# A two-layer hybrid decoder step on one core: the second part of the tokens as one 512-column product, gate_a through Silu

## The chip, the core and the metric

The kernel runs on one core of a Trainium2 chip. The core has five engines with an instruction queue each, and each queue runs strictly in its order: PE (TensorE, the matrix products; PEld is its loading of weights), DVE (VectorE), ACT (ScalarE), POOL (GpSimd) and SP (here the queue that issues most transfers). Matrix products land in PSUM; DVE and ACT read them from there. The metric is the device time of one launch in microseconds (us), smaller is better; times of single instructions are also given in nanoseconds (ns).

## The reference

One inference step of two layers over 512 prompt tokens and 8 sample tokens, all in float32, with 1024 channels. Per layer:

```python
h = rms_norm(x, norm_g)
z = h @ w_in                       # 50 blocks of 128 columns: glu 16, k, v, q 8, gate_b 8, mg_b 8, mg_a 8 (and gate_a 8)
u = glu[..., :1024] * sigmoid(glu[..., 1024:])
c = conv(concat([conv_buf, u]), conv_w) + conv_b           # 31 taps, each channel by itself
c = silu(layer_norm(c, ln_g, ln_b)) * silu(gate_a)
y_a = c @ w_conv_out
o, new_k, new_v = attend(rope(q), rope(k), v, sinks)       # window of 128, 16 heads, 2 kv heads
y_b = (o * silu(gate_b)) @ w_attn_out
y = sigmoid(mg_a) * y_a + sigmoid(mg_b) * y_b
x = x + y @ w_out
```

After the two layers comes a last rms_norm. The last 30 conv inputs and the last 128 keys and values go out too.

## The kernel before

Channels lie on the partitions and the 520 tokens along the free axis, so that an activation is 8 tiles of 128 x 520. Weights come in blocks of 1024 x 128. One such block with its product over all tokens is a `Unit`; there are 82 in a layer, 164 in all: 16 GLU, K, V, 8 Q, 8 gate_b (GB), 16 merge gates (MB, MA), 8 gate_a (GA), 8 YB, 8 YA, 8 OUT.

To hold float32 accuracy with products of the reduced type `fp32r`, weights and activations are split into a high and a low part (`whi` and `wlo`; a pair of tiles for each activation), and three products are summed: high x high, low weight x high, high weight x low activation. `Unit.__init__` loads the weights over SP (`raw`), ACT casts them to `whi` (line 109) and DVE subtracts to get `wlo` (line 110). `raw` has two buffers, `whi` and `wlo` three each. The tokens are done in two halves of 260; each half of a unit is 8 blocks of input channels times 3 products of 260 columns, 48 in a unit, all on line 124, into one PSUM bank per half. `mm` pairs of banks exist twice, so the results of a unit have to be read before the next unit but one begins. A single ACT copy or DVE operation over 520 columns does that, according to the unit's kind.

The attention of a layer goes in 32 steps (`scores`, `transposes`, `values`), with half a unit of MB or MA between two steps. The depthwise convolution is 240 DVE operations per layer (line 563, 30 taps for each of 8 tiles) with a low priority, put in wherever DVE has room. Its end is followed by a layer norm: a sum over channels, which is a matrix product with `ones` (line 160, reading `ssum`), the subtraction of the mean (577), squares, a second sum, then the scale (581), Silu (602) and the product with gate_a (604). The result is needed by the YA units.

The order on each engine is written by a list scheduler when the program is built. It works with its own estimates of time and the priorities; on the chip each queue is then fixed, and an instruction whose input is late holds up everything behind it in its queue.

Of the kernel before, what the change touches and what calls it, by code (L numbers as in the profile page):

```python
# [19 lines left out]
HALF = TOK // 2  # L20
# [23 lines left out]
def hybrid_step(ctx, tc, x_in, w_in, par, const, rope, conv_st, kc_in, vc_in,  # L44
# [6 lines left out]
    gp = ctx.enter_context(tc.tile_pool(name="gp", bufs=42))  # L51
# [16 lines left out]
    def g(dt=F32):  # L68
        return gp.tile([128, TOK], dt, tag="g", name=name("g"))

    def og(dt=F32):
        return gp.tile([128, TOK], dt, tag="o", bufs=16, name=name("o"))

    def two(t):
        return t.rearrange("p (a b) -> p a b", a=2)
# [18 lines left out]
    def split(src, n=TOK, new=g):  # L94
        hi, lo = new(F32R), new(F32R)
        A.copy(hi[:, :n], src)
        mark[0] = V.tensor_tensor(lo[:, :n], src, hi[:, :n].bitcast(F32), op=ALU.subtract)  # L97
        return hi, lo

    class Unit:  # L100


        def __init__(self, l, idx, hs, los, spare=False):
            self.hs, self.los = hs, los
# [6 lines left out]
            if spare:  # L111
                banks = [psT.tile([128, 512], F32, tag="T", name=name("T")),
                         psV.tile([128, 512], F32, tag="V", name=name("V"))]
                self.acc = [b[:, :HALF] for b in banks]
# [12 lines left out]
        def half(self, hf):  # L127
            for k in range(KT):
                self.step(hf, k)
            return self.acc[hf]  # L130

        def both(self):
            self.half(0)
            self.half(1)
            return self.ps

    class Sum:
# [6 lines left out]
        def add(self, i, v, halves=(0, 1)):  # L144
            if i == 7 and len(halves) == 1:
                self.left[halves[0]] = two(v)[:, halves[0], :]
                return
            c = slice(halves[0] * HALF, (halves[-1] + 1) * HALF)
# [8 lines left out]
        def total(self, hf):  # L157
            ps = sbank()[:, :HALF]
            last = self.left.get(hf)
            PE.matmul(ps, ones, two(self.acc)[:, hf, :], start=True, stop=last is None)  # L160
# [7 lines left out]
    def rstd(sums, halves=(0, 1)):  # L168
        y0, v, a = tmp("y0", 1), tmp("v", 1), tmp("a", 1)
        c = slice(halves[0] * HALF, (halves[-1] + 1) * HALF)  # L170
        for hf, s in zip(halves, sums):
            h = slice(hf * HALF, (hf + 1) * HALF)
# [22 lines left out]
    def first_units(l):  # L195
        return [Unit(l, W_GLU, xh, xl), Unit(l, W_GLU + 1, xh, xl)]

    def rows(x, i):

        w = pt[:, P_G + i:P_G + i + 1]  # L200
        a, b = g(F32R), g(F32R)
        A.mul(a, x, w)  # L202
        mark[0] = V.scalar_tensor_tensor(b, x, w, a.bitcast(F32), op0=ALU.mult, op1=ALU.subtract)
        xh.append(a)
        xl.append(b)
# [5 lines left out]
    xs, xh, xl, sq = [], [], [], Sum()  # L211
    first = []
    xt = [g() for _ in range(KT)]
    for i in range(KT):
        if i < 2:
            first.append(Unit(0, W_GLU + i, xh, xl))
# [6 lines left out]
    for l in range(L):  # L223
# [6 lines left out]
        hh, hl = [], []  # L230

        def normed(lo, hi):
            for i in range(lo, hi):
# [3 lines left out]
                a, b = split(h)  # L237
                hh.append(a)
                hl.append(b)
# [3 lines left out]
        for i in range(KT):  # L243
            if i % 2 == 0:
# [3 lines left out]
            src = (xh, xl) if i < EARLY else (hh, hl)  # L248
            if i == 0:
                for k in range(KT):  # L250
                    for u in first:
                        u.step(0, k)
                        u.step(1, k)
                R = rstd(sq.totals())
                a, b = first
            else:
                a = Unit(l, W_GLU + 2 * i, *src, spare=(i == 1))
                a.half(0)
                a.half(1)
            u = up.tile([128, PAD + TOK], F32, tag="u", name=f"u{l}_{i}")  # L260
            G.memset(u[:, :PAD], 0.0)
            uu = two(u[:, PAD:])
            sg = g()
            if i < EARLY:
                for hf in range(2):
                    A.copy(two(sg)[:, hf, :], a.acc[hf])
                if i > 0:
                    b = Unit(l, W_GLU + 2 * i + 1, *src)
                    b.both()
                A.copy(uu, b.ps)  # L270
# [4 lines left out]
                V.tensor_tensor(uu, uu, two(sg), op=ALU.mult)  # L275
            else:
                A.activation(two(sg), a.ps, AF.Sigmoid)
                z1 = Unit(l, W_GLU + 2 * i + 1, *src).both()
                V.tensor_tensor(uu, z1, two(sg), op=ALU.mult)
# [23 lines left out]
        kps = Unit(l, W_K, hh, hl).both()  # L303
        kn, kcos, ksin, krot = g(), g(), g(), g()
        nc.gpsimd.dma_start(kcos, rope[2])
        nc.gpsimd.dma_start(ksin, rope[3])
        A.copy(two(kn), kps)
        V.tensor_tensor(krot, kn, kcos, op=ALU.mult)
        vps = Unit(l, W_V, hh, hl).both()
        vt = g()  # L310
        A.copy(two(vt), vps)
        nc.gpsimd.dma_start(nvp[l], vt[:, T - 128:T])
        for hf in range(2):
            c = slice(hf * HALF, (hf + 1) * HALF)
            kss = sbank()
            PE.matmul(kss[:, :HALF], swap, kn[:, c], start=True, stop=True)
            V.tensor_tensor(ksin[:, c], kss[:, :HALF], ksin[:, c], op=ALU.mult)
# [3 lines left out]
        for kv in range(2):  # L321
            a, b = g(F32R), g(F32R)
# [8 lines left out]
        for j in range(2):  # L331
            t = g()
# [9 lines left out]
        cosx, sinx = g(), g()  # L342
# [3 lines left out]
        def q_store(e, src):  # L346
            a, b = split(src[:, :T], T)
            for j, t in ((0, a), (HD, b)):
                nc.sync.dma_start(qscr[:, j + 8 * e:j + 8 * e + 8, :], t[:, :T].bitcast(F32))
            nc.gpsimd.dma_start(qsam[:, 8 * e:8 * e + 8, :], src[:, T:])  # L350

        x1p = Unit(l, W_Q, hh, hl).both()
        x1, x1c, x1s = g(), g(), g()
        A.copy(two(x1), x1p)
# [6 lines left out]
        vb = g()  # L361
# [3 lines left out]
        vrow = g()  # L365
# [4 lines left out]
        for j in range(2):  # L370
            t = g()
# [6 lines left out]
        x2p = Unit(l, W_Q + 1, hh, hl).both()  # L378
        x2, x2c, x2s = g(), g(), g()
        A.copy(two(x2), x2p)  # L380
        for e in range(2, 8):
            q = Unit(l, W_Q + e, hh, hl).both()
            qe = tmp("sq", 3)
            A.copy(two(qe), q)
# [8 lines left out]
        qn = g()  # L393
        qn3 = qn[:, :128].rearrange("p (t v n) -> p t v n", t=8, v=2)
        G.memset(qn[:, :128], 0.0)
# [7 lines left out]
        def load_q(t):  # L403
            for kv in range(2):
                q = g(F32R)
                nc.sync.dma_start(q[:, :T].bitcast(F32), qscr[2 * t + kv])
                qs[t, kv] = q

        sgb = []
        for t in range(8):  # L410
            ps = Unit(l, W_GB + t, hh, hl).both()
            s = g()
            A.activation(two(s), ps, AF.Silu)  # L413
            sgb.append(s)
# [7 lines left out]
        def sample_scores():  # L422
            ss = sbank()
            for j in range(2):
                qb = g()
                G.memset(qb[:, :512], 0.0)
                qb3 = qb[:, :512].rearrange("p (n m) -> p n m", n=4)
                for n in range(4):
                    nn = 4 * j + n
                    V.tensor_copy(qb3[:, n, nn * 16:nn * 16 + 16],  # L430
                                  qn[:, :128].rearrange("p (h n) -> p h n", n=NS)[:, :, nn])
                    PE.matmul(ss[:, :128], qb3[:, n, :], kc[j][:, n, :],  # L432
                              start=(nn == 0), stop=(nn == 7))
            ns = g()
# [356 lines left out]
```

## Time and profile before

| | |
|---|---|
| time of three runs | 1074.34 to 1075.82 us, median 1075.18 |
| the profiled execution's own time | 1074.0 us |
| its span from the first to the last instruction | 1072.2 us |
| granted TensorE clock, mean | 0.997 of full speed |
| PE busy | 1053.9 us, 98% of the span |
| DVE busy | 854.2 us, 80% |
| ACT busy | 514.0 us, 48% |

A share of busy time is an average over stages. Products are pipelined on PE: the record of one lasts longer than the distance to the next one's start, and this distance (its pitch) is what a product costs in a dense run. The same holds on a smaller scale on DVE.

### The profile page before, as it was taken

Reading aid. Unit: us, or ns where it says so; the run is one execution under the profiler, and the core shown is the slowest. Engines: PE = TensorE matmul, PEld = TensorE weight load, DVE = VectorE, ACT = ScalarE, POOL = GpSimd, SP = SyncE. Lnnn points to the kernel's source line nnn. Section 1 sums busy time; section 2 is a strip of 40 time slices with the busy share of each in tenths; the row PEclk is TensorE's granted clock in tenths of the full one; section 3 lists DMA queues with packets and bytes.
Section 4 is the critical chain, followed back from the end, with each engine's and each line's share of the span. In section 5 each row is a group of like instructions: output and inputs, shape, how many; then the busy total and the mean of one; then the engine's idle time right before and its main releaser. Section 6 shows DMA issues by size and latency. Waiting matters only on the chain.

```text
span 1072.2 us, 21484 instructions
## 1 busy us (share of the span) xinstructions
PE 1053.9 (98%) x8724; PEld 1032.2 (96%) x8724; DVE 854.2 (80%) x1568; ACT 514.0 (48%) x949; POOL 79.3 (7%) x185
## 2 busy tenths in 40 slices
PE   7999999999999999999999999999999999999996
PEld 7999999999999999999999999999999999999995
DVE  5999999999999587455569999999999976944545
ACT  6622443356666785224453234334666686822321
POOL 1011221000001100000101013100000000000000
PEclk9999999999999999999999999999999999999998
DMA  5443574332222225223334337633232313252312
GB/s 218 130 129 111 168 253 149 101 117 80 99 82 72 68 70 189 95 99 113 134 99 139 119 119 247 201 103 119 80 116 67 95 41 99 86 175 96 98 60 80
DMA packets 44115, 126.41 MB, mean 118 GB/s; under 512 B 6176, under 2 KB 8816, under 8 KB 44016
## 3 DMA queue, kind: packets, MB, share of 16 engines
q1 hardware_dynamic: 37440, 110.23, 31.3%
q0 software_dynamic: 5136, 13.45, 3.9%
q8 instruction: 68, 1.11, 0.4%
q10 hardware_dynamic: 1440, 1.37, 0.4%
q14 instruction: 31, 0.25, 0.1%
HBM read 107.66 MB, written 17.36 MB: 117 GB/s over the span
## 4 chain that ended last, share of the span: by engine, by line
PE 95%; DVE 3%; DMA 1%; ACT 0%; issue 0%; SPq 0%; DVEq 0%; ACTq 0%
PE mm L124 85%; PE S L474 3%; PE pv L509 3%; PE PT L500 2%; DMA raw<-w 1%; PE T L124 1%; DVE g L663 1%; DVE wlo L110 1%; DVE sq L235 1%; PE S L160 0%; DVE g L97 0%; PE S L432 0%; PE pvs L454 0%; PE V L124 0%; ACT whi L109 0%
## 5 line engine op out<-in xcount | busy, mean ns | idle before, releaser
L124 PE MATMUL mm<-g,whi 128*128 128x260 f32 x4160 | 771.3, 284 | 7.6 <-ACT g L202 7.0
L124 PEld LDWEIGHTS mm<-g,whi 128*128 128x128 f32 x4160 | 646.3, 188 | 14.4 <-ACT g L202 7.4
L124 PE MATMUL mm<-g,wlo 128*128 128x260 f32 x2080 | 589.2, 284 | 0.0
L124 PEld LDWEIGHTS mm<-g,wlo 128*128 128x128 f32 x2080 | 393.1, 189 | 1.0 <-issue 0.8
L563 DVE SCALAR_TENSOR_TENSOR acc<-u,par,acc 128x512 f32<-128x512 f32 x464 | 329.6, 746 | 0.2
L109 ACT CAST whi<-raw 128x1024 fp32r<-128x1024 f32 x164 | 172.2, 1050 | 206.7 <-PE mm L124 167.3
L110 DVE TENSOR_TENSOR wlo<-raw,whi 128x1024 fp32r<-128x1024 f32 x164 | 200.4, 1223 | 55.3 <-ACT whi L109 55.1
L124 PE MATMUL mm<-o,whi 128*128 128x260 f32 x992 | 178.9, 282 | 0.4 <-DVE g L652 0.4
L124 PEld LDWEIGHTS mm<-o,whi 128*128 128x128 f32 x992 | 153.0, 188 | 0.6 <-DVE g L652 0.6
L124 PE MATMUL mm<-o,wlo 128*128 128x260 f32 x496 | 139.5, 282 | 0.0
L124 PEld LDWEIGHTS mm<-o,wlo 128*128 128x128 f32 x496 | 93.2, 188 | 0.0
L486 ACT ACTIVATE p<-p,sm 128x257 f32<-128x257 f32 (+1 forms) x128 | 60.9, 478 | 12.4 <-DVE sm L480 12.3
L502 ACT COPY pts<-PT 128x256 f32<-128x256 f32 (+1 forms) x64 | 33.8, 528 | 62.1 <-PE PT L500 61.9
L480 DVE CUSTOM_DVE_ANT_0 p<-S,con,nsk 128x256 f32<-128x256 f32 (+1 forms) x128 | 52.6, 448 | 10.9 <-PE PT L500 9.3
L478 POOL COPY p<-nsk 128x2 f32<-128x2 f32 x64 | 23.4, 369 | 360.8 <-PE PT L500 284.3
L615 DVE TENSOR_TENSOR g<-mm,g 128x520 f32<-128x520 f32 x16 | 11.2, 700 | 42.9 <-PE mm L124 42.9
L474 PE MATMUL S<-g,g 128*128 128x256 f32 x256 | 42.1, 284 | 0.0
L609 DVE TENSOR_TENSOR g<-mm,g 128x520 f32<-128x520 f32 x16 | 11.2, 699 | 32.0 <-PE mm L124 32.0
L413 ACT ACTIVATE g<-mm 128x520 f32<-128x520 f32 x16 | 9.7, 607 | 55.9 <-PE mm L124 55.9
L500 PE MATMUL PT<-con,p 128*128 128x128 f32 x224 | 35.6, 276 | 0.0
L474 PEld LDWEIGHTS S<-g,g 128*128 128x128 f32 x256 | 35.2, 189 | 0.4 <-DVE sm L480 0.4
L490 ACT ACTIVATE p<-p,sm 128x128 f32<-128x128 f32 (+1 forms) x64 | 29.8, 479 | 6.4 <-DVE sm L489 6.4
(167 smaller groups left out, 817.0 us busy)
## 6 DMA issues: line engine op xcount, KB each, us to landing
raw<-w SPq DMA_DIRECT2D x164, 512.0 KB, 3.4
qscr<-g SPq DMA_DIRECT2D x32, 256.0 KB, 4.5
g<-qscr SPq DMA_DIRECT2D x32, 256.0 KB, 3.7
g<-x SPq DMA_DIRECT2D x16, 260.0 KB, 7.2
g<-rope POOLq DMA_DIRECT2D x8, 260.0 KB, 4.0
xres<-g POOLq DMA_DIRECT2D x8, 260.0 KB, 2.3
g<-xres SPq DMA_DIRECT2D x8, 260.0 KB, 4.3
g<-conv_state POOLq DMA_DIRECT2D x8, 248.0 KB, 3.4
```

The costliest lines, as they stand in the source:

```text
L109: A.copy(self.hi, raw)
L110: V.tensor_tensor(self.lo, raw, self.hi.bitcast(F32), op=ALU.subtract)
L124: PE.matmul(self.acc[hf], a[:, k, :], b[k][:, c], start=(k == 0 and j == 0), stop=(k == KT - 1 and j == 2))
L474: PE.matmul(S3[:, kv, :], qs[t, kv][:, b * 128:b * 128 + 128], K[kv][:, k0:k0 + 256], start=(j == 0), stop=(j == 1))
L478: G.tensor_copy(p[:, :, nk:nk + 1], nsk[:, 2 * t:2 * t + 2].unsqueeze(2))
L480: V.tensor_tensor_reduce(out=p[:, kv, :nk], in0=S3[:, kv, :nk], in1=con[:, C_MASK + 256 - nk:C_MASK + 256], op0=ALU.add, op1=ALU.min, scal ...
L486: exp_ins[0] = A.activation(p[:, kv, :nk + 1], p[:, kv, :nk + 1], AF.Exp, bias=nm[:, kv:kv + 1], scale=-1.0, accum_out=dn[:, kv:kv + 1])
L490: A.mul(p[:, 0, :nk], p[:, 0, :nk], dn[:, 0:1])
L500: PE.transpose(PT[:, kv, kb, :], p[:, kv, kb * 128:kb * 128 + 128], ident)
L502: A.copy(pts[t][:, :, j0:j0 + nb, :], PT[:, :, :nb, :])
L509: PE.matmul(pv[kv * 64:kv * 64 + 64, j * 128:(j + nb) * 128], vb[:, j * 128 + kv * 64:j * 128 + kv * 64 + 64], pts[t][:, kv, 2 * j:2 * j + ...
L563: V.scalar_tensor_tensor(dst, us[i][:, k:k + T], cw(i, k), acc[i], op0=ALU.mult, op1=ALU.add)
```

## The change

The tokens are cut at 264 instead of 260 (`NX, NY = 264, 256`). The high and the low part of an activation now lie in one tile of 128 x 2 x 520. The first 264 tokens are done as before, with 24 products of 264 columns. For the other 256 tokens the high and the low part stream through the high weights as one product of 512 columns (`second`, part 0) that fills a whole PSUM bank: 256 sums of high x high and 256 of high x low side by side. The low weights then add 8 products of 256 columns onto the first of the two. So a unit has 40 products for 48, over the same 12,480 columns. The two sums are added when the results are read: either by one DVE operation after the copy (`add_low`), or by an ACT copy and a DVE addition in PSUM ahead of the reader (`fold`). A layer has 42 folds (10 GLU, 8 each of GB, GA, YB, YA) and 40 of `add_low`.

gate_a, which was copied out, passed through a Sigmoid and multiplied with itself on DVE, now goes through one Silu straight from PSUM, ordered behind the last exponential of the attention. Other tiles are packed in twos, without a change of what is computed from them.

```diff
-HALF = TOK // 2
+NX, NY = 264, 256
+X, Y = slice(0, NX), slice(NX, TOK)
+CS = (X, Y)
...
     def split(src, n=TOK, new=g):
-        hi, lo = new(F32R), new(F32R)
-        A.copy(hi[:, :n], src)
-        mark[0] = V.tensor_tensor(lo[:, :n], src, hi[:, :n].bitcast(F32), op=ALU.subtract)
-        return hi, lo
+        t = new(F32R)
+        A.copy(t[:, 0, :n], src)
+        mark[0] = V.tensor_tensor(t[:, 1, :n], src, t[:, 0, :n].bitcast(F32), op=ALU.subtract)
+        return t
...
-                mm = mmp.tile([128, 2, 512], F32, tag="mm", name=name("mm"))
-                self.ps = mm[:, :, :HALF]
-                self.acc = [self.ps[:, 0, :], self.ps[:, 1, :]]
-
-        def step(self, hf, k):
-            c = slice(hf * HALF, (hf + 1) * HALF)
-            for j, (a, b) in enumerate(((self.hi, self.hs), (self.lo, self.hs),
-                                        (self.hi, self.los))):
-                PE.matmul(self.acc[hf], a[:, k, :], b[k][:, c],
+                mm = mmp.tile([128, 2, 512], F32, tag="mm", name=name("mm"))
+                mm = mm.rearrange("p a b -> p (a b)")
+                self.ps = mm[:, 512 - NX:512 + NY]
+                a, b = mm[:, 512 - NX:512], mm[:, 512:]
+            self.acc = (a, b[:, :NY])
+            self.low = b[:, NY:2 * NY]
+            self.pair = b.rearrange("p (a b) -> p a b", a=2)
+
+        def first(self, k):
+            for j, (a, part) in enumerate(((self.hi, 0), (self.lo, 0), (self.hi, 1))):
+                PE.matmul(self.acc[0], a[:, k, :], self.hs[k][:, part, X],
                           start=(k == 0 and j == 0), stop=(k == KT - 1 and j == 2))
 
+        def second(self, k, part):
+            if part == 0:
+                PE.matmul(self.pair, self.hi[:, k, :], self.hs[k][:, :, Y],
+                          start=(k == 0), stop=False)
+            else:
+                PE.matmul(self.acc[1], self.lo[:, k, :], self.hs[k][:, 0, Y],
+                          start=False, stop=(k == KT - 1))
...
+        def fold(self):
+
+            t = tmp("low", 2, NY)
+            A.copy(t, self.low)
+            V.tensor_tensor(self.acc[1], self.acc[1], t, op=ALU.add)
             return self.ps
+
+        def copy(self, dst):
+            A.copy(dst, self.ps)
+            self.add_low(dst)
+
+        def add_low(self, dst):
+            V.tensor_tensor(dst[:, Y], self.low, dst[:, Y], op=ALU.add)
...
-        sga = []
+        sga = row(KT)
         for i in range(KT):
-            ps = Unit(l, W_GA + i, hh, hl).both()
-            s = g()
-            A.copy(two(s), ps)
-            sga.append(s)
+            ps = Unit(l, W_GA + i, hp).both().fold()
             with tc.issue_after(exp_ins[0].ins):
+                A.activation(sga[i], ps, AF.Silu)
+        with tc.issue_after(exp_ins[0].ins):
+            for i in range(KT):
                 A.activation(mgb[i], mgb[i], AF.Sigmoid)
                 A.activation(mga[i], mga[i], AF.Sigmoid)
-                sg = tmp("sq", 3)
-                A.activation(sg, s, AF.Sigmoid)
-            V.tensor_tensor(s, s, sg, op=ALU.mult)
```

The change moves instructions in the queues too. On PE before, the sum of the layer norm of layer 0 (`S594`, `S595`) stands right behind the second GA unit (`mm619`) and ahead of the transposes `PT577`:

```order
L124 MATMUL mm619_4599<-g93_602,whi617_4595 128x260
L124 MATMUL mm619_4599<-g93_602,wlo618_4596 128x260
L124 MATMUL mm619_4599<-g94_603,whi617_4595 128x260
L160 MATMUL S594_4470<-ssum592_4461,ones_88 128x260
L160 MATMUL S595_4472<-ssum592_4461,ones_88 128x260
L500 MATMUL PT577_4170<-con_87,p553_4011 128x128 x4
L124 MATMUL mm625_4661<-g50_305,whi623_4657 128x260
```

On PE after, the same sum (`S536`, `S537`) stands within the third GA unit (`mm569`):

```order
L526 MATMUL PT522_3793<-con_87,p513_3732 128x128 x4
L136 MATMUL mm569_4253<-g57_412,whi567_4249 128x264
L136 MATMUL mm569_4253<-g70_534,whi567_4249 128x264
L136 MATMUL mm569_4253<-g70_534,wlo568_4250 128x264
L136 MATMUL mm569_4253<-g70_534,whi567_4249 128x264
L136 MATMUL mm569_4253<-g72_539,whi567_4249 128x264
L197 MATMUL S536_4080<-ssum534_4071,ones_88 128x264
L197 MATMUL S537_4082<-ssum534_4071,ones_88 128x256
L136 MATMUL mm569_4253<-g72_539,wlo568_4250 128x264
L136 MATMUL mm569_4253<-g72_539,whi567_4249 128x264
L141 MATMUL mm569_4253<-g37_278,whi567_4249 128x512
L141 MATMUL mm569_4253<-g39_283,whi567_4249 128x512
```

So the sum moved back by 22 products of a unit, and 12 transposes and 2 rows of `values` that stood behind it now stand ahead of it.

On DVE before, this is the end of the convolution of layer 0 (`u0_6` and `u0_7` are its last two tiles, `ssum592` the sum that `S594` reads):

```order
L563 SCALAR_TENSOR_TENSOR u0_6_1038<-u0_6_1038,par0_92,acc590_4397 128x512
L491 TENSOR_SCALAR p559_4059<-p559_4059,sm561_4061 128x256
L489 RECIPROCAL sm570_4114<-sm570_4114 128x2
L563 SCALAR_TENSOR_TENSOR acc591_4398<-u0_7_1155,par0_92,acc591_4398 128x512
L514 TENSOR_TENSOR sq573_4158<-pv572_4149,g274_2328 128x512
L517 TENSOR_TENSOR sq581_4197<-g330_2670,g279_2385 64x8 x2
L155 TENSOR_TENSOR ssum592_4461<-ssum592_4461,u0_6_1038 128x520
L491 TENSOR_SCALAR p568_4112<-p568_4112,sm570_4114 128x256
L563 SCALAR_TENSOR_TENSOR u0_7_1155<-u0_7_1155,par0_92,acc591_4398 128x512
L155 TENSOR_TENSOR ssum592_4461<-ssum592_4461,u0_7_1155 128x520
```

On DVE after, the same end, with the fold of the second GA unit (`mm564`) and weights of a later unit (`wlo578`) within it:

```order
L107 TENSOR_TENSOR o518_3774<-sq517_3770,o518_3774 128x520
L588 SCALAR_TENSOR_TENSOR u0_6_935<-u0_6_935,par0_92,acc532_4007 128x512
L588 SCALAR_TENSOR_TENSOR acc533_4008<-u0_7_1042,par0_92,acc533_4008 128x512
L121 TENSOR_TENSOR wlo578_4352<-raw576_4349,whi577_4351 128x1024
L192 TENSOR_TENSOR ssum534_4071<-ssum534_4071,u0_6_935 128x520
L164 TENSOR_TENSOR mm564_4202<-mm564_4202,low565_4243 128x256
L588 SCALAR_TENSOR_TENSOR u0_7_1042<-u0_7_1042,par0_92,acc533_4008 128x512
L192 TENSOR_TENSOR ssum534_4071<-ssum534_4071,u0_7_1042 128x520
```

The convolution has the same 240 operations. Ahead of its end DVE now also has 52 of the new additions over 256 columns (20 folds, 32 of `add_low`), two more subtractions for `wlo` (55 for 53) and one more split of an attention output (line 107).

## Rows read from the trace of the kernel before

**Rows 1.** The page: span, busy time and share of three engines.

```profile
span 1072.2 us, 21484 instructions
...
PE 1053.9 (98%) x8724; PEld 1032.2 (96%) x8724; DVE 854.2 (80%) x1568; ACT 514.0 (48%) x949; POOL 79.3 (7%) x185
```

**Rows 2.** The page: the chain that ended last, by engine.

```profile
PE 95%; DVE 3%; DMA 1%; ACT 0%; issue 0%; SPq 0%; DVEq 0%; ACTq 0%
```

**Rows 3.** Windows: stretch, length, busy time (instructions), clock, DMA share, GB/s.

```profile
core 0: us, PE busy (x) PEld busy (x) DVE busy (x) ACT busy (x) POOL busy (x), PEclk, DMA share, GB/s
0.00:32.00 32.00, 24.93 (x183) 24.06 (x184) 20.10 (x31) 19.22 (x29) 3.02 (x19) 1.00 0.60 215
...
32.00:75.00 43.00, 42.47 (x356) 42.26 (x354) 43.00 (x73) 19.52 (x30) 4.86 (x9) 1.00 0.40 124
75.00:200.00 125.00, 125.00 (x1045) 124.86 (x1044) 117.07 (x172) 43.76 (x60) 18.66 (x35) 1.00 0.50 159
200.00:353.00 153.00, 153.00 (x1276) 145.15 (x1275) 143.97 (x368) 95.88 (x244) 9.84 (x29) 1.00 0.27 91
353.00:442.00 89.00, 89.00 (x740) 87.57 (x739) 56.51 (x77) 54.22 (x81) 4.72 (x11) 1.00 0.34 114
442.00:545.00 103.00, 103.00 (x865) 103.00 (x864) 52.11 (x65) 33.66 (x43) 4.89 (x9) 1.00 0.33 111
```

**Rows 4.** Waits of PE, longest total first.

```profile
PE mm L124 <- ACT g L202: 7.0, 1, 7.0
PE S L162 <- ACT sq L654: 0.6, 1, 0.6
```

**Rows 5.** The chain in order of time: start us, us, what.

```profile
356.76 0.88 PE S L160 x4
...
366.10 0.44 PE PT L500 x4
366.53 0.58 PE pv L509 x4
...
387.51 157.98 PE mm L124 x1323
```

**Rows 6.** Timeline of PE: start us, us from first start to last end.

```profile
230.20 1.86 PE L454 MATMUL pvs<-g,g 128*128 128x16 f32 x16
...
303.77 0.63 PE L474 MATMUL S<-g,g 128*128 128x256 f32 x4
```

**Rows 7.** Groups of DVE by form: count, busy us, mean ns, idle before.

```profile
L110 DVE TENSOR_TENSOR wlo<-raw,whi 128x1024 fp32r<-128x1024 f32 x164 | 200.4, 1223 | 55.3 <-ACT whi L109 55.1
...
L595 DVE TENSOR_TENSOR g<-g,sq 128x520 f32<-128x520 f32 x16 | 10.6, 695 | 0.0
...
L652 DVE TENSOR_TENSOR g<-mm,g 128x260 f32<-128x260 f32 x14 | 5.9, 427 | 17.7 <-PE mm L124 17.7
```

**Rows 8.** Timeline of DVE around the end of the convolution.

```profile
352.25 0.70 DVE L155 TENSOR_TENSOR ssum<-ssum,u 128x520 f32<-128x520 f32 x1
...
363.40 4.97 DVE L577 TENSOR_TENSOR u<-u,a 128x520 f32<-128x520 f32 x8
```

**Rows 9.** Waits of DVE from 32 to 353 us: total, times, longest.

```profile
DVE wlo L110 <- ACT whi L109: 7.6, 12, 1.1
DVE p L480 <- PE PT L500: 4.9, 7, 1.2
DVE sq L514 <- PE pv L509: 1.9, 5, 0.7
DVE u L279 <- PE mm L124: 1.2, 3, 0.6
```

**Rows 10.** Groups of ACT by form.

```profile
L588 ACT COPY g<-mm 128x520 f32<-128x520 f32 x16 | 9.4, 588 | 8.4 <-PE mm L124 8.4
...
L594 ACT ACTIVATE sq<-g 128x520 f32<-128x520 f32 x16 | 9.7, 635 | 0.6 <-DVE ssum L155 0.6
...
L266 ACT COPY g<-mm 128x260 f32<-128x260 f32 x8 | 2.6, 378 | 15.3 <-PE mm L124 15.3
```

**Rows 11.** Timeline where YA passes into OUT in layer 0.

```profile
490.71 0.70 DVE L97 TENSOR_TENSOR o<-g,o 128x520 fp32r<-128x520 f32 x1
...
492.92 0.40 PE L124 MATMUL mm<-o,wlo 128*128 128x260 f32 x2
```

**Rows 12.** Timeline of the last unit's reading.

```profile
1060.83 0.42 DVE L652 TENSOR_TENSOR g<-V,g 128x260 f32<-128x260 f32 x1
```

More of the change, by code (lines that the diff above doesn't have):

```diff
@@ L68, in g, with couple, row @@
     def g(dt=F32):
-        return gp.tile([128, TOK], dt, tag="g", name=name("g"))
+        return gp.tile([128, 2, TOK], dt, tag="g", name=name("g"))
     def og(dt=F32):
-        return gp.tile([128, TOK], dt, tag="o", bufs=16, name=name("o"))
-    def two(t):
-        return t.rearrange("p (a b) -> p a b", a=2)
+        return gp.tile([128, 2, TOK], dt, tag="o", bufs=8, name=name("o"))
+    def couple():
+        t = g()
+        return t[:, 0, :], t[:, 1, :]
+    def row(n):
+        return [t for _ in range(n // 2) for t in couple()]
     def sbank():
@@ new lines, in second @@
+        def second(self, k, part):
[5 more added lines that the diff above has]
+                          start=False, stop=(k == KT - 1))
+        def half(self, hf):
+            if hf == 0:
+                for k in range(KT):
+                    self.first(k)
+            else:
+                for part in range(2):
+                    for k in range(KT):
+                        self.second(k, part)
+            return self
@@ L145, in add @@
             if i == 7 and len(halves) == 1:
-                self.left[halves[0]] = two(v)[:, halves[0], :]
+                self.left[halves[0]] = v[:, CS[halves[0]]]
                 return
-            c = slice(halves[0] * HALF, (halves[-1] + 1) * HALF)
+            c = slice(CS[halves[0]].start, CS[halves[-1]].stop)
             if i == 0:
@@ L157, in total @@
         def total(self, hf):
-            ps = sbank()[:, :HALF]
+            ps = sbank()[:, :CS[hf].stop - CS[hf].start]
             last = self.left.get(hf)
-            PE.matmul(ps, ones, two(self.acc)[:, hf, :], start=True, stop=last is None)
+            PE.matmul(ps, ones, self.acc[:, CS[hf]], start=True, stop=last is None)
             if last is not None:
@@ L210, in hybrid_step @@
     log_exp()
-    xs, xh, xl, sq = [], [], [], Sum()
+    xs, xp, sq = [], [], Sum()
     first = []
-    xt = [g() for _ in range(KT)]
+    xt = row(KT)
     for i in range(KT):
         if i < 2:
-            first.append(Unit(0, W_GLU + i, xh, xl))
+            first.append(Unit(0, W_GLU + i, xp))
         nc.sync.dma_start(xt[i], x_in[:, i, :])
@@ L251, in hybrid_step @@
                     for u in first:
-                        u.step(0, k)
-                        u.step(1, k)
+                        u.first(k)
+                        u.second(k, 0)
+                        u.second(k, 1)
                 R = rstd(sq.totals())
@@ L330, in hybrid_step @@
         kc = []
-        for j in range(2):
-            t = g()
+        for j, t in enumerate(couple()):
             c4 = t[:, :512].rearrange("p (n s) -> p n s", n=4)
@@ L369, in hybrid_step @@
         vc = []
-        for j in range(2):
-            t = g()
+        for j, t in enumerate(couple()):
             c4 = t[:, :512].rearrange("p (n s) -> p n s", n=4)
@@ L403, in load_q @@
         def load_q(t):
+            q = g(F32R)
             for kv in range(2):
[L405 to L409, printed above, removed]
+                nc.sync.dma_start(q[:, kv, :T].bitcast(F32), qscr[2 * t + kv])
+                qs[t, kv] = q[:, kv, :]
+        sgb = row(8)
         for t in range(8):
[L411 to L414, printed above, removed]
+            A.activation(sgb[t], Unit(l, W_GB + t, hp).both().fold(), AF.Silu)
             if t == 3:
@@ L423, in sample_scores @@
             ss = sbank()
-            for j in range(2):
-                qb = g()
+            for j, qb in enumerate(couple()):
                 G.memset(qb[:, :512], 0.0)
@@ L517, in values @@
                 V.tensor_tensor(o[r, T:], smp["o"][r, :, 2 * t + kv], sgb[t][r, T:], op=ALU.mult)
-            a, b = split(o, new=og)
-            oh.append(a)
-            ol.append(b)
+            op.append(split(o, new=og))
         LAG = 3
@@ L573, in hybrid_step @@
         for hf, s in enumerate(sm.totals()):
-            A.mul(two(mu)[:, hf, :], s, -1.0 / D)
+            A.mul(mu[:, CS[hf]], s, -1.0 / D)
         sm = Sum()
```

209 lines of the change are left out of this document (99 added, 110 removed).

## The prediction

> **What bounds the kernel now.** I start with the shares of the page: PE is busy for 1053.9 of 1072.2 us, DVE for 854.2 [rows 1]. The chain that ended last says the same, 95% of it on PE [rows 2]. PE's own waits come to little: 7.0 us at the start, then 0.6 us [rows 4]. So as it stands, a nanosecond off each product is a nanosecond off the end. The windows show what the average hides, and here the reader should look longest: from 32 to 353 us DVE is busy for 43.00 + 117.07 + 143.97 = 304.0 of 321 us, in the first stretch without a gap, while from 353 us on it is busy for little over half the time [rows 3]. In the first part of each layer there are thus two engines near their limit, in the second part one. What the change takes from PE and gives to DVE has to be costed for the two parts separately.
>
> **What it takes from PE.** The columns of a unit are the same, 12,480, so a gain can only come from what a product costs beyond its columns. 1323 products of 260 columns follow each other in 157.98 us [rows 5], which is 119.4 ns each; other dense runs give up to 120.0, and I use 119.8. At the full clock of 2.4 GHz, which the windows grant (1.00) [rows 3], 260 columns are 108.3 ns, so 11.5 ns lie on top. Four products of 256 columns start 0.63 − 0.28 = 0.35 us apart in all, 117 ns each [rows 6], in line with 119.8 less 4 columns (118.1). So 264 columns cost 121.5 and 256 cost 118.
>
> No product of 512 columns runs before. Bounds: at worst it costs what two of 256 do, 236 ns, and nothing is gained. If the 11.5 ns stay on top once, it is 213.3 + 11.5 = 224.8. The row nearest in length is the sum with `ones`: 4 passes in 0.88 us [rows 5], 220 ns for a pass. That pass has 260 float32 columns and takes twice their 108.3 = 216.7, which leaves only 2 to 3 ns on top, though each pass loads weights of its own. With that a 512-column product would cost 215.6. Where do the 11.5 ns come from? 16-column products are still (1.86 − 0.26) / 15 = 107 ns apart [rows 6], so loading weights has a floor of about that; products of 256 to 264 columns are so close to it that load and stream get in each other's way, which a longer product would hide. But the nearest row streams at half rate, so I take 220, between 215.6 and 224.8.
>
> A unit: 24 x 121.5 + 8 x 220 + 8 x 118 = 5620 ns, against 48 x 119.8 = 5750. That is 130 ns a unit (165 with 215.6, 92 with 224.8, nothing with 236), and 164 units make 21.3 us (27, 15, 0).
>
> The Trainium skill, "TensorE: Matmul & The Clock Gate", section "Back-to-back issue gap", gives a warm gap of N / 2.4 + 2.5 ns. By it 8 products fewer would save 20 ns a unit, 3.3 us in all, as an estimate from that page. The trace does not agree at 260 columns (119.8 against 110.8), so I don't use it for the sum.
>
> **What it gives to DVE.** 82 additions over 256 columns a layer. The nearest row, 260 columns with one operand in PSUM, records 427 ns [rows 7]; but 8 operations of 697 ns fit into 4.97 us [rows 8], a pitch of 0.61, so some 0.09 of each record overlaps the next. I take 0.34 us. Removed: 8 multiplications of gate_a a layer (0.61 each) [rows 7], behind the end of the convolution, where DVE has room. ACT gets 42 copies of 256 columns a layer (378 ns for 260) and loses 8 copies and 8 Sigmoids for 8 Silus [rows 10]; at 48% busy it hides that, and I charge nothing.
>
> **The first part of a layer.** PE's queue has one place where it must wait for the convolution: the layer-norm sum. Before, `ssum` was finished at 352.25 + 0.70 = 352.95 and PE reached the sum at 356.76 [rows 5, 8], 3.8 us later. The order shown with the change puts it 22 products further on (2.67 us) and behind 12 transposes and 2 rows of `values` (3 x 0.44 + 0.44 to 0.58 us by [rows 5], taken as 1.8 together). So the same place in the work was passed at 361.2 before. PE alone would now get there 52 units x 0.13 = 6.8 us earlier, at 354.4.
>
> DVE has 304.0 us of work up to there, plus 52 additions (17.7), two `wlo` (2.3) and one split (0.6): 324.6 us. Without any gap that ends at 356.6; with all 17 us of gaps that it has now, at 373.6. The gaps are named: 7.6 us for ACT's cast of weights, 8.0 for PE's transposes, values and units [rows 9]. Waits for PE vanish when PE is ahead, and ACT's cast waits for weight buffers that PE frees; on the other side each fold brings a new wait for ACT's copy. I leave 5 us, and the sum starts at 361.7: 7 us later than PE alone could, and 0.5 us later than before at the same place. So I expect the first part to gain nothing from 52 units. Queued behind the waiting sum are all later GA units. The wait will probably be spread, partly in the attention, where a product of scores needs a bank that DVE still has to read. I charge nothing for the clock: the 7.0 us wait at the start stands in a window that is granted 1.00 [rows 3].
>
> **The second part.** From there on 29.45 units run with DVE at 56.5 of 89 and 52.1 of 103 us [rows 3]. The YA units need the convolution branch; the new order leaves the chain to it as long as before, and I charge nothing. Where YA passes into OUT the last split ended at 491.4 and PE needed it at 492.9 [rows 11]; copy and fold (0.38 + 0.34, about 0.9 with the handovers) fit into these 1.5 us, and nothing is left if they take twice that. So PE keeps 29.45 x 0.13 = 3.8 us. At the very end the last reading is one more operation on the path, 0.4 us [rows 12].
>
> **Sum.** Two layers of +0.5 − 3.8 make −6.6; +0.4 at the end; −6.2. The profiled execution took 1074.0, 1.2 below the median of the runs, so 1075.2 − 6.2 = 1069.
>
> **Rivals.**
>
> *DVE keeps up.* It works without gaps, as it does from 32 to 75 us [rows 3], or the scheduler's order spreads its work well enough that PE decides everywhere. Then the whole 21.3 us show: 1054 (1048 with 215.6). Against it: the sum above, which leaves PE's 354.4 out of DVE's reach even without a gap.
>
> *DVE falls behind: slower.* One mechanism, at the sum. If the gaps of before stay, it starts at 373.6, 12.4 us late; less 3.8 that is 8.6 a layer, 17.6 with the end: 1093. The point that decides is 8.3 us of gaps in the first part of a layer: above it the kernel is slower. For it: 94.1% is what DVE reaches in the attention [rows 3], with short operations that wait for PE and ACT in turns.
>
> *The long product costs as much as two.* Whatever lies on top grows with the columns. Then PE alone is at the sum at 361.2 and DVE at 361.7, the second part gains nothing, and 2 x 0.5 + 0.4 gives 1077. For it: no row shows a full-rate stream longer than 264 columns. If only 2.5 ns a product are saved, the second part gains 0.6 us a layer and the time is 1075, no change.
>
> **How the numbers follow.** My forecast has 0.42, DVE keeping up 0.20, DVE falling behind 0.18, a long product without gain 0.15, the last case 0.05. What a measurement can tell from no change is about 0.2%, 2.15 us: below 1073.0 is faster, above 1077.3 slower. My forecast, 3 us wide either way for the gaps and 5 for the price of a product, is faster in 0.29, the same in 0.09 and slower in 0.04. DVE keeping up is faster in all 0.20, falling behind slower in 0.17 and the same in 0.01, the long product slower in 0.08, the same in 0.06 and faster in 0.01; the last case goes 0.02, 0.02 and 0.01. That makes 0.52, 0.18, 0.30. The likeliest case's own range is 1064 to 1076; for 8 in 10 it must take in most of DVE keeping up and the milder half of falling behind: 1052 to 1085.
>
> **What would show it.** In the changed profile: products of 512 columns about 220 ns apart in a dense run; a unit of 5.62 us where nothing is waited for; DVE from 32 to 353 us at 98% or more; PE with waits for `ssum` or for DVE in the attention of some 7 us a layer, which it does not have now; the distance from the first layer-norm sum to the end of the layer 3.8 us shorter. It would be wrong if the long product costs under 216 or over 225 ns, or if DVE's gaps are far from 5 us.

## The result, and the profile after

The changed kernel takes 1111.85 us (1110.99 to 1113.27) where the one before took 1075.2 in the median on the same chip: a ratio of 1.0343 [1.0323, 1.0363], 37 us slower. One execution of the kernel before, of 2012.83 us, is left out of its median and of the ratio. The forecast was 1069, its range ended at 1085.

The page of the kernel after, span and busy time:

```profile
span 1111.5 us, 19233 instructions
...
PE 1066.3 (96%) x7412; PEld 978.5 (88%) x7412; DVE 900.6 (81%) x1716; ACT 545.7 (49%) x1025; POOL 82.6 (7%) x185
```

Against [rows 1] PE issues 1312 products fewer, and yet it is busy for 12.4 us more and idle for 26.9 us more (45.2 against 18.3). Those two make the 39.3 us of the span. Windows of the kernel after: stretch, length, busy times, granted clock:

```profile
32.00:75.00 43.00, 41.77 (x287) 38.56 (x286) 42.99 (x75) 20.23 (x33) 3.79 (x7) 1.00 0.36 112
75.00:200.00 125.00, 124.63 (x870) 116.39 (x869) 118.13 (x190) 49.41 (x72) 19.69 (x37) 1.00 0.52 162
200.00:353.00 153.00, 152.16 (x1106) 136.21 (x1105) 145.74 (x373) 96.61 (x241) 12.59 (x28) 1.00 0.28 90
347.00:470.00 123.00, 113.53 (x760) 103.80 (x759) 78.84 (x124) 65.23 (x110) 2.64 (x13) 0.94 0.28 91
888.00:1011.00 123.00, 113.81 (x764) 103.99 (x764) 79.66 (x127) 65.73 (x111) 0.59 (x1) 0.94 0.28 91
```

The last two rows run, for each layer, from the last product of scores to the first sum of the two branches (`mga` plus `mgb`), to about a microsecond. In the kernel before the same stretches are:

```profile
342.00:449.00 107.00, 107.00 (x888) 104.45 (x887) 70.09 (x107) 65.83 (x103) 6.05 (x13) 1.00 0.31 105
866.00:974.00 108.00, 108.00 (x895) 105.50 (x894) 69.36 (x107) 66.36 (x105) 0.36 (x1) 1.00 0.32 107
```

Before, PE never pauses there. After, the two are 16 and 15 us longer, 31 of the 39: PE is idle for 9.5 and 9.2 us, and the clock of 0.94 takes up to 0.06 x 123 = 7.4 from each. They begin where the attention ends and hold the layer norm, the GA units and the YB units. The waits of PE in the kernel after name what it waits for (total, times, longest):

```profile
PE PT L526 <- ACT pts L528: 11.2, 4, 3.8
PE mm L136 <- ACT g L613: 7.5, 2, 3.8
PE mm L136 <- ACT g L239: 7.4, 1, 7.4
PE S L197 <- DVE ssum L192: 2.3, 1, 2.3
```

L239 is the wait at the start, as in [rows 4]. The other two are new, and neither is for `ssum` (that row is the final norm's). The two new ones together are 18.7 of the 26.9 us.

First the transposes: the one bank for PT is read by a copy (L528) that stands in ACT's queue behind the Sigmoids of `mgb` and `mga`. ACT and PE of the kernel after, timeline:

```profile
354.84 1.28 ACT L616 ACT_TABLE_LOAD   x1
...
362.49 0.62 ACT L616 ACTIVATE g<-g 128x520 f32<-128x520 f32 x1
363.01 0.35 ACT L528 COPY pts<-PT 128x256 f32<-128x256 f32 x1
...
366.05 1.03 ACT L120 CAST whi<-raw 128x1024 fp32r<-128x1024 f32 x1
366.98 0.36 ACT L163 COPY low<-mm 128x256 f32<-128x256 f32 x1
367.24 0.58 ACT L528 COPY pts<-PT 128x512 f32<-128x512 f32 x1
...
363.41 0.66 PE L526 MATMUL PT<-con,p 128*128 128x128 f32 x4 [1.92 <-ACT pts L528]
367.88 1.11 PE L526 MATMUL PT<-con,p 128*128 128x128 f32 x4 [3.81 <-ACT pts L528]
```

The copy of 367.24, which the longer wait is for, stands behind three more Sigmoids, a cast of weights and a copy for a fold (L163). And in PE's queue these two groups of four transposes follow each other directly, both into that one bank. In the kernel before 67 products of units stand between the two groups there:

```profile
357.48 0.60 PE L500 MATMUL PT<-con,p 128*128 128x128 f32 x4
...
365.93 0.60 PE L500 MATMUL PT<-con,p 128*128 128x128 f32 x4
```

Then the gate. This is the chain back from a GA product at 407.40, in order of time (start us, us, what):

```profile
395.36 0.85 ACT sq L210 x2
...
397.51 0.65 ACT sq L213
...
400.27 1.22 DVE wlo L121
401.49 4.88 DVE u L606 x8
406.37 0.35 DVE mm L164
...
406.75 0.61 ACT g L613
...
407.40 4.77 PE mm L136 x20
```

The next unit needs the bank of an earlier GA unit. To free it takes a copy on ACT (L163, done by 399.36), the addition on DVE (L164) and the Silu on ACT (L613). The addition stands behind the eight multiplications of the layer norm (L606), which wait for the square root's steps: 7 us go by between copy and addition, and PE stands still for 3.74 us. Before, one ACT copy freed the bank, and no unit waited there.

### The profile page after: what moved, and what is told of

The parts are those of the page before. It is cut to its first block, busy times and chain, and to the rows that moved or that the text cites. A ratio compares the mean times of both kernels' runs of the same rounds, so it can differ in the third digit from the quotient of the medians.

```text
span 1111.5 us, 19233 instructions
## 1 busy us (share of the span) xinstructions
PE 1066.3 (96%) x7412; PEld 978.5 (88%) x7412; DVE 900.6 (81%) x1716; ACT 545.7 (49%) x1025; POOL 82.6 (7%) x185
## 4 chain that ended last, share of the span: by engine, by line
PE 90%; ACT 5%; DVE 3%; issue 1%; DMA 0%; DVEq 0%; ACTq 0%
PE mm L136 42%; PE mm L141 26%; PE mm L144 13%; PE S L500 3%; PE pv L535 3%; PE PT L526 2%; DVE u L606 1%; ACT whi L120 1%; PE T L136 1%; ACT g L616 1%; ACT g L617 1%; DVE g L684 1%; PE V L141 1%; PE S L197 0%; DMA raw<-w 0%
## 5 line engine op out<-in xcount | busy, mean ns | idle before, releaser
L136 PE MATMUL mm<-g,whi 128*128 128x264 f32 x2080 | 423.0, 290 | 18.7 <-ACT g L613 7.5
L136 PEld LDWEIGHTS mm<-g,whi 128*128 128x128 f32 x2080 | 340.7, 192 | 28.0 <-ACT g L613 9.4
L136 PE MATMUL mm<-g,wlo 128*128 128x264 f32 x1040 | 300.2, 289 | 0.0
L141 PE MATMUL mm<-g,whi 128*128 128x512 f32 x1040 | 273.2, 397 | 0.0
L141 PEld LDWEIGHTS mm<-g,whi 128*128 128x128 f32 x1040 | 187.1, 189 | 32.8
L136 PEld LDWEIGHTS mm<-g,wlo 128*128 128x128 f32 x1040 | 199.9, 192 | 0.3
L144 PEld LDWEIGHTS mm<-g,wlo 128*128 128x128 f32 x1040 | 143.6, 189 | 11.4 <-issue 0.3
L144 PE MATMUL mm<-g,wlo 128*128 128x256 f32 x1040 | 151.2, 281 | 0.0
L136 PE MATMUL mm<-o,whi 128*128 128x264 f32 x496 | 95.8, 284 | 0.1
L136 PE MATMUL mm<-o,wlo 128*128 128x264 f32 x248 | 70.5, 285 | 0.0
L528 ACT COPY pts<-PT 128x256 f32<-128x256 f32 (+1 forms) x64 | 33.9, 530 | 64.9 <-PE PT L526 64.7
L141 PE MATMUL mm<-o,whi 128*128 128x512 f32 x248 | 62.3, 393 | 0.4 <-DVE g L673 0.4
L526 PE MATMUL PT<-con,p 128*128 128x128 f32 x224 | 37.5, 284 | 11.2 <-ACT pts L528 11.2
L136 PEld LDWEIGHTS mm<-o,wlo 128*128 128x128 f32 x248 | 46.6, 188 | 0.0
(176 smaller groups left out, 1111.5 us busy)
```

The lines of the kernel that those rows point to most:

```text
L136: PE.matmul(self.acc[0], a[:, k, :], self.hs[k][:, part, X], start=(k == 0 and j == 0), stop=(k == KT - 1 and j == 2))
L141: PE.matmul(self.pair, self.hi[:, k, :], self.hs[k][:, :, Y], start=(k == 0), stop=False)
L144: PE.matmul(self.acc[1], self.lo[:, k, :], self.hs[k][:, 0, Y], start=False, stop=(k == KT - 1))
L526: PE.transpose(PT[:, kv, kb, :], p[:, kv, kb * 128:kb * 128 + 128], ident)
L528: A.copy(pts[t][:, :, j0:j0 + nb, :], PT[:, :, :nb, :])
```

## The experiments

"Idle" is span less PE's busy time on the page of the run's profile. The list scheduler writes the queues anew for each run, so that a run can differ from the kernel after by more than its edit. Where that shows, the text says so.

| run | us | ratio to before | span | PE busy | idle |
|---|---|---|---|---|---|
| before | 1075 | 1 | 1072.2 | 1053.9 | 18.3 |
| after | 1111.85 | 1.0343 [1.0323, 1.0363] | 1111.5 | 1066.3 | 45.2 |
| e1_gate_copy | 1112.49 | 1.0348 [1.0333, 1.0363] | 1110.9 | 1064.1 | 46.8 |
| e2_silu_alone | 1080.22 | 1.0046 [1.0031, 1.0061] | 1077.4 | 1055.1 | 22.3 |
| e3_no_additions | 1083.03 | 1.0073 [1.0058, 1.0088] | 1080.8 | 1054.4 | 26.4 |
| e4_two_products | 1100.43 | 1.0243 [1.0224, 1.0263] | 1098.9 | 1062.5 | 36.4 |
| e5_copy_no_additions | 1088.28 | 1.0121 [1.0106, 1.0136] | 1087.7 | 1056.9 | 30.8 |
| e6_additions_ahead_only | 1092.22 | 1.0158 [1.0143, 1.0173] | 1089.8 | 1057.5 | 32.3 |
| e7_additions_behind_only | 1099.78 | 1.0225 [1.0208, 1.0242] | 1098.1 | 1060.5 | 37.6 |
| e8_fewer_taps | 1096.71 | 1.0197 [1.0182, 1.0212] | 1095.4 | 1058.6 | 36.8 |
| e9_sigmoids_behind | 1112.74 | 1.0353 [1.0331, 1.0376] | 1108.9 | 1062.3 | 46.6 |
| e10_no_gate_additions | 1094.72 | 1.0184 [1.0169, 1.0199] | 1092.5 | 1060.0 | 32.5 |
| e12_gate_bank_by_ACT | 1099.95 | 1.0229 [1.0212, 1.0246] | 1098.8 | 1064.0 | 34.8 |
| e13_both_moves | 1100.44 | 1.0244 [1.0229, 1.026] | 1101.6 | 1062.6 | 39.0 |

**Gate_a read as before.** The kernel after with copy, Sigmoid and product in place of Silu.

```diff
-            ps = Unit(l, W_GA + i, hp).both().fold()
...
+            Unit(l, W_GA + i, hp).both().copy(s)
...
```

> The changed kernel with gate_a read as before: one ACT copy out of PSUM with the addition behind it, then Sigmoid and the product with itself on DVE. ACT theory (the 36 us are lost because ACT's queue, around the GA units, holds PSUM banks and the copies of the transposes behind Silus, Sigmoids and their table loads): PE no longer waits for a Silu of gate_a, one of the two stalls of 4 us in each layer and the drop of the clock behind it go, 1085 to 1098 us. DVE theory (the 164 additions make the convolution end 18 us later, whoever reads gate_a): DVE has 16 products more to do, the end of the convolution stays at 369 us, 1108 to 1118 us.

No gain. The longer wait at the transposes goes (3.8 us in all in place of 11.2): PE's queue has 34 products between the two groups here. But the gate's stall grows by about as much. It only changes its reader: the bank now waits for `add_low` on DVE, behind the same eight multiplications, once a layer and longer. Timeline of PE in this run, and its waits:

```profile
413.42 0.59 PE L136 MATMUL mm<-o,whi 128*128 128x264 f32 x1 [8.49 <-DVE g L172]
...
PE mm L136 <- DVE g L172: 18.2, 6, 8.5
```

**Silu alone**, in the kernel before: `A.activation(two(s), ps, AF.Silu)` right from the bank.

> The kernel before with gate_a alone through one Silu out of PSUM, ordered behind the last exponential; products and halves as before. ACT theory: the Silu alone brings waits of PE for it, 1080 to 1095 us. DVE theory: DVE has 16 products less and nothing more, the convolution ends at 352 us as before, 1073 to 1077 us.

It costs 5 us by itself: the Silu comes behind the last exponential and a table load, so the banks are read later than by a copy; PE waits for it 4 times, 1.2 us at most.

**No additions.** `fold` and `add_low` do nothing, so the products of high weights and low activations of the last 256 tokens are computed and not added.

> The changed kernel without the additions of the two sums and the copies ahead of them: the product of high weights and low activations is left out of the result for the last 256 tokens. DVE theory: with 52 additions less in the first part of a layer the convolution ends near 352 us, the stalls of PE go, 1070 to 1078 us (the long products at 232 ns save 5 us at most). ACT theory: gate_a still goes through Silu out of PSUM behind other work, 1085 to 1100 us.

29 us come back, and the clock stays at 1.00 in both stretches. PE's waits at the transposes are gone too. So most of the loss comes with the additions; 8 us stay, and the time lies between the two expectations.

**Short products again.** Seven of the eight 512-column products of a unit as two of 256, additions kept.

```diff
-            if part == 0:
+            if part == 0 and k == 0:
...
```

> The changed kernel with 7 of the 8 long products of each unit done as two of 256 columns into the same places (47 products in a unit in place of 40); additions, Silu and the cut at 264 stay. By the pitches of the changed profile (232 ns for 512 columns, 118 for 256) PE does 28 ns a unit more, 4.6 us: 1112 to 1118 us. If the long product were worth the 130 ns a unit that was forecast, 1128 us or more. If the place of the loss is in queues that wait anyway, part of it hides and the time stays within 2 us of 1112.

With 1148 products more it is 11 us *faster* than the kernel after, outside all three expectations. PE is idle for 8.8 us less: its waits at the transposes go from 11.2 to 4.6 us, in a queue of ACT whose first Sigmoids stand at 348 us in place of 355, and the clock falls less (1.00 in the stretch of the second layer). The edit touches no reader of a bank, so a shift of the stalls alone can be worth 11 us here. The long product is worth less than that.

**The products alone**: no additions (the same part left out) and gate_a by a copy.

> Gate_a read as before (copy, Sigmoid, product) and none of the added additions (the product of high weights and low activations is left out for the last 256 tokens); the 512-column products stay. It is the change's work on TensorE alone. Theory long-product-gives-nothing (pitch 232 ns against 2 x 118): 1073 to 1077 us, the time before. Rival, the forecast's 16 ns a pair: 1052 to 1060 us.

PE's busy time of 1056.9, and of 1054.4 in e3_no_additions, against 1053.9 before, confirms that the long product gives nothing. The total missed the expectation by 11 us. From 871 to 988 us PE is idle for 6 us at a clock of 0.97, in the first layer's stretch for 2.7 at 1.00. One wait there (2.8 us) is for the copy of a GA bank, which stands behind Sigmoids in ACT's queue; ACT switches tables there between Sigmoid and Exp, 1.28 us each time. The other (3.2) is for a reading of YB's bank on DVE, which stands behind the eight multiplications of the layer norm. So a bank is read late in this place even with no addition at all.

**Additions on one side only.** In the two runs additions are made only ahead of gate_a (`idx < W_GA`) or only in GA, YB, YA and OUT; elsewhere the same product is left out.

> The kernel after with the additions kept only in the units ahead of gate_a (GLU, K, V, Q, GB, MB, MA), and left out in GA, YB, YA and OUT. Theory VectorE-late (the additions ahead of the convolution's last tap move the layer-norm sum by some 17 us a layer): 1105 to 1112 us, with the falls of the granted clock at 365 and 406 us still there. Rival gate-reader (the additions at GA and behind it hold the banks): 1083 to 1092 us.

> The reverse: additions only in GA, YB, YA and OUT, none in the units ahead. Theory VectorE-late: 1083 to 1090 us, convolution done near 351 us, no fall of the clock. Rival gate-reader: 1103 to 1112 us.

Both theories miss their numbers, and the second is nearer. Over the run without any addition the 50 additions ahead cost 9 us, the 32 behind 17, though those lie where DVE is busy for less than two thirds of the time. Together that is 26 of 29 us.

**Fewer taps.** All additions stay; 28 of 240 tap instructions a layer are left out (`if k in (5, 15, 25) or (k == 20 and i % 4 < 2): continue`).

> The kernel after with all its additions, but 28 of the 240 tap instructions of each layer left out (28 x 0.743 = 20.8 us of VectorE work a layer; taps 5, 15, 25 of each tile and 20 of half of them do not enter the convolution). Theory VectorE-late: the convolution is done near 350 us again and the time is 1078 to 1088 us. Rival, that the additions cost by what they do to a bank or to TensorE and not by VectorE's time: over 1100 us.

Neither number holds. The last tap ends at 334.9 us, against 370.1 in the kernel after, and the sum starts at 347.49. Still the time is 22 us over the kernel before, and PE waits in the gate:

```profile
394.39 0.39 PE L136 MATMUL mm<-g,whi 128*128 128x264 f32 x1 [2.65 <-ACT g L615]
```

With the last `ssum` addition done 34 us earlier than after, and 16 earlier than before, 15 us come back. Since DVE is relieved by more than the additions cost it, a late DVE is at most that part of the loss, and not the whole.

**Sigmoids behind the copies**, in the kernel after.

```diff
-                exp_ins[0] = A.activation(p[:, kv, :nk + 1], p[:, kv, :nk + 1], AF.Exp,
...
+                A.activation(p[:, kv, :nk + 1], p[:, kv, :nk + 1], AF.Exp,
...
-            A.copy(pts[t][:, :, j0:j0 + nb, :], PT[:, :, :nb, :])
+            exp_ins[0] = A.copy(pts[t][:, :, j0:j0 + nb, :], PT[:, :, :nb, :])
```

> The kernel after; only the Sigmoids and Silus of the gates are ordered behind the last copy of the transposed probabilities instead of behind the last exponential. Theory reader-chain (the loss lies in PE's stalls behind the attention, where what PE needs stands late in ScalarE's or VectorE's queue): the stalls at the transposes near 361 and 364 us (6.1 us a layer) go, the one in the gate stays: 1093 to 1103 us. Rival VectorE-late: no gain, 1109 to 1116 us.

The waits of the transposes go, and the time stays. PE's waits in this run:

```profile
PE mm L136 <- ACT g L613: 18.5, 9, 4.0
```

They went over to the gate's Silu, which was ordered behind the same copies: 18.5 instead of 7.5 us. My expectation counted the two stalls as independent; they share ACT's queue.

**No additions in GA.** 8 of 82 a layer (the same part left out there); Silu reads the bank.

> The kernel after without the additions of the eight gate_a units a layer (their product of high weights and low activations is left out for the last 256 tokens); Silu reads the bank directly. All other additions stay. Theory reader-chain: PE's wait in the gate goes from 3.8 us to under 1.5, the transposes' stalls stay: 1090 to 1100 us. Rival, all 82 additions count alike by VectorE's time: 8/82 of 29 us, 1107 to 1111 us.

17 us come back (1.0343 less 1.0184), 1.07 us for each of 16 additions, whose own records are 0.425 us. Windows of the two stretches in this run:

```profile
347.00:461.00 114.00, 110.82 (x766) 101.81 (x765) 76.74 (x117) 65.54 (x104) 2.83 (x13) 0.99 0.31 99
879.00:992.00 113.00, 109.81 (x758) 100.87 (x757) 75.75 (x116) 65.38 (x104) 0.60 (x1) 0.98 0.31 99
```

Each is 9 or 10 us shorter than after: 3.2 us idle instead of 9, a clock of 0.99 and 0.98. The last tap came no earlier (it ends at 372.2 us, after 370.1), so it is not VectorE's load ahead of it that these 17 us come from. Nor are they the gate's alone. PE is idle for 12.7 us less, and its waits name the places: 5.0 us in the GA units (2.5 for 7.5), and 7.4 at the transposes (3.8 for 11.2), which the expectation took to stay. PE's queue now has 51 products between the two groups:

```profile
363.54 0.66 PE L529 MATMUL PT<-con,p 128*128 128x128 f32 x4 [1.92 <-ACT pts L531]
365.45 0.39 PE L137 MATMUL mm<-g,whi 128*128 128x264 f32 x1 [1.26 <-ACT g L616]
374.00 0.60 PE L529 MATMUL PT<-con,p 128*128 128x128 f32 x4
```

**The gate's bank freed by ACT alone.** The same work, with both parts copied out by ACT, the addition and Silu in SBUF.

```diff
-            ps = Unit(l, W_GA + i, hp).both().fold()
+            u = Unit(l, W_GA + i, hp).both()
...
+            A.copy(s, u.ps)
+            A.copy(lows[i % 4], u.low)
+            V.tensor_tensor(s[:, Y], s[:, Y], lows[i % 4], op=ALU.add)
...
-                A.activation(sga[i], ps, AF.Silu)
+                A.activation(s, s, AF.Silu)
```

> The kernel after; in the gate_a units ScalarE copies both parts out of the bank, and addition and Silu work in SBUF, so the bank comes free by one engine's queue. Same VectorE work, one more ScalarE copy of 520 columns a unit. Theory reader-chain: PE's wait in the gate goes, 1090 to 1101 us, the transposes' stalls stay. Rival, it is the amount of work and not the hops: 1109 to 1118 us.

12 us come back with every addition still made and one ACT copy more. Here too PE's queue has products (42) between the two groups of transposes, and their waits go from 11.2 to 3.8 us; so against the kernel after the route of the bank and the order of PE's queue change together. The run to compare with is e1_gate_copy, which also takes the Silu off the bank and has products between the transposes, but frees the bank by an ACT copy and a DVE addition. Its PE waits 18.2 us for that addition; in this run PE's waits in the GA and YB units are these:

```profile
PE mm L136 <- ACT g L106: 2.4, 3, 1.9
PE mm L136 <- ACT g L617: 2.0, 2, 1.0
PE mm L136 <- DVE g L636: 1.7, 1, 1.7
```

Together 6.1 us in place of 17.5 (18.2 less the 0.7 that both runs have elsewhere), and the times lie 12.5 us apart. With the same additions made, what costs there is mostly the way through DVE's queue and not the work. Part of the difference can come from the 16 products on DVE and the Sigmoids that e1_gate_copy has besides.

**Both moves.**

> Both moves together: gate bank freed by ScalarE alone, and Sigmoids and Silus behind the last copy of the transposed probabilities. All of the change's work is done. Theory reader-chain: no stall over 2 us is left behind the attention, the granted clock stays at 1.00, 1076 to 1086 us. Rival VectorE-late: 1100 to 1112 us.

No better than the one alone. Part of the waiting goes one step further, to where YB's bank is read by DVE (L636) behind the same chain:

```profile
421.11 0.36 PE L136 MATMUL mm<-o,whi 128*128 128x264 f32 x1 [3.72 <-DVE g L636]
```

## Why the prediction was wrong

**The step that failed** is in "What it gives to DVE": each addition was priced by the time that it occupies DVE, and for ACT's copies and the Silus the text says "at 48% busy it hides that, and I charge nothing". PE's two new waits are both for ACT, 11.2 us at the transposes and 7.5 at the gate, 18.7 of the 26.9 us that PE is idle more; from 361 to 366 us ACT is busy for 5.00 of 5 us. What decides is what stands ahead in ACT's and DVE's queues at the time, not their occupation.

At the transposes, the copy that frees the one bank stands behind Sigmoids, casts and a fold's copy, while PE's queue has two groups of transposes one behind the other. In the gate, a bank that one ACT copy freed is now freed by ACT, then DVE, then ACT, through two queues that work in order and hold the layer norm at that time. Of the eight GA additions a layer two were priced at 0.34 us and six at nothing, since they lie behind the convolution's end. Without the eight the time is 17 us shorter (e10_no_gate_additions). Between the two profiles it is 19.0: 5.0 in the waits of the GA units, 7.4 in those of the transposes, and 6.3 in PE's busy time, at a higher clock. That a bank's way through DVE's queue can cost more than the addition is seen in e12_gate_bank_by_ACT against e1_gate_copy: 12.5 us. How much of the 37 us is the route of the gate's banks, and how much the order that the scheduler wrote, stays open: no run changes the one and keeps the other.

**"I charge nothing for the clock."** The 7 us wait at the start was the wrong row to judge by: PE had run nothing yet, and the window's 1.00 does not show what follows it. Timeline of PE in the kernel before:

```profile
10.43 0.64 PE L124 MATMUL mm<-g,whi 128*128 128x260 f32 x2
10.86 0.42 PE L124 MATMUL mm<-g,wlo 128*128 128x260 f32 x1
11.08 0.59 PE L124 MATMUL mm<-g,whi 128*128 128x260 f32 x2
```

Three products in 11.08 − 10.43 = 0.65 us are 217 ns each, 260 / 1.2: the half level, in the trace that the forecast was made from. In the kernel after the stalls of 3.5 to 3.8 us are each followed by a lower clock; windows of the first layer, around its stalls:

```profile
361.00:366.00 5.00, 1.15 (x9) 0.71 (x7) 4.03 (x8) 5.00 (x11) 0.50 (x1) 0.98 0.00 0
366.00:372.00 6.00, 4.12 (x17) 3.04 (x18) 4.78 (x8) 4.70 (x8) 0.19 (x1) 0.50 0.27 87
...
407.00:413.00 6.00, 5.60 (x25) 5.60 (x26) 4.54 (x8) 2.81 (x5) 0.12 (x1) 0.50 0.26 87
414.00:420.00 6.00, 6.00 (x43) 5.60 (x42) 3.68 (x6) 4.76 (x9) 0.25 (x2) 1.00 0.21 67
```

PE was busy for 1.15 of 5 us, then the granted clock is 0.50, the 1.2 GHz level. The two stretches lose up to 14.8 us by it (0.06 x 246), enough for the 12.4 that PE's busy time grew.

**The long product**, 220 ns by estimate, was mis-sized. A unit in the YB part of the kernel after (timeline of PE; the first row is its first product):

```profile
415.98 0.28 PE L136 MATMUL mm<-o,whi 128*128 128x264 f32 x1
...
418.92 2.02 PE L141 MATMUL mm<-o,whi 128*128 128x512 f32 x8
420.78 1.12 PE L144 MATMUL mm<-o,wlo 128*128 128x256 f32 x8
421.73 0.28 PE L136 MATMUL mm<-o,whi 128*128 128x264 f32 x1
```

(420.78 − 418.92) / 8 is 232.5 ns for 512 columns, against 2 x 119 for two of 256. The unit takes 421.73 − 415.98 = 5.75 us, as 48 products of before at 119.4 to 120 do (5.73 to 5.76). That is the third rival's case: the cost on top grows with the columns. By the Trainium skill, "TensorE: Matmul & The Clock Gate", section "Back-to-back issue gap", which gives its rule for a product by itself, 512 columns would take 215.8 ns, as an estimate from that page; the trace is 17 ns above it. The float32 row that I leaned on says nothing of a full-rate stream, and a longer product does not hide what lies on top, as I had supposed. So the 21 us that PE could have gained were never there.

**The first part of a layer.** The work was sized right (from 32 to 370 us DVE is busy for 321.3, and 0.8 us of the last sum's addition follow, against 324.6 forecast). From 32 to 353 us it is busy for 306.9 of 321, 95.6%, where I wrote 98% or more. The gaps were mis-sized: 338 − 321.3 = 16.7 us, where I left 5 and before had 17. DVE's waits for PE fell from 8.0 to 4.4 us and did not vanish, since PE did not run ahead; those for ACT rose from 7.6 to 9.7. The last `ssum` addition ends at 370.81 us, 17.9 us later than in [rows 8].

**The rival "DVE falls behind"** had this gap and the sign. It put the end of `ssum` and the sum at 373.6; the sum starts at 374.4, but that is luck. `ssum` was done at 370.8, and PE reached the sum 3.6 us after that, late by its stalls at the transposes and the lower clock behind them. The rival's mechanism, PE waiting at the sum, did not happen: PE's only wait for `ssum` is at the end. The layer norm makes itself felt some 30 us further on, where GA's banks are read. A DVE far ahead of before takes back 15 us and leaves a stall there (e8_fewer_taps).

**Sum of the loss**, taking things away in turn: GA's additions 17, the other additions 12 (1094.7 − 1083.0), the rest 8 (e3_no_additions). These are differences between runs whose queues differ too, and not prices that add up: in the kernel before the Silu alone costs 5, yet with a copy in its place and no additions the rest is 13 and not 3 (e5_copy_no_additions). No run beats the kernel before.

The second part's −3.8 us a layer fell with the product's price. The tail's +0.4 was too small: PE waits 2.3 us for the last `ssum`, where before its one wait in the last norm was 0.6 [rows 4].

## What to carry to other kernels

Where matmul banks rotate, cost an edit at a bank's reader by the route that frees it: how many engines, and what stands ahead in each queue at that time. An engine at 50% on average gives no cover when Sigmoids or the chain of a norm hold it just then. Look in PE's queue for two users of one bank with nothing between them. A gain that rests on a longer instruction wants one measured at that length, or is no gain.

## What the runs showed of the hardware

At the granted clock of 0.50 a 264-column product takes (411.97 − 408.01) / 18 = 220 ns, which is 264 / 1.2 with nothing on top; at 1.00 it takes 122, 12 above 264 / 2.4. What is on top at full clock does not show at the half level, and it grows with the columns: 12 ns at 256 and at 264, 19 at 512. PE timeline of the kernel after, at the half level:

```profile
408.01 0.64 PE L136 MATMUL mm<-g,whi 128*128 128x264 f32 x2
...
411.97 0.42 PE L136 MATMUL mm<-g,whi 128*128 128x264 f32 x1
```

So a stall can cost more than its length: behind that of 3.74 us in the first layer, 6 us at the half level lose 3 more.
